# A decoder layer on one core: the router stage in another order, x1's low halves on VectorE, and x1's halves stored in plain column order

## The chip, the cores and the metric

The kernel runs on one core of a Trainium2 chip. A core has five engines with an instruction queue each: TensorE (PE; its weight loads are listed apart as PEld), VectorE (DVE), ScalarE (ACT), GpSimd (POOL) and SyncE (SP, which here issues nearly all DMA transfers). Each engine works through its own queue in program order; semaphores make an engine wait for another. The metric is the device time of one execution in microseconds (us). Most executions of one kernel lie close together, and a difference under 2% is hard to tell from none.

## What is computed

The reference is one layer of a decoder for 512 tokens of width 1024, in float32: a mixer of mLSTM heads and windowed attention, a residual with layer norm, and a mixture of 32 experts in 4 groups (the best group, then the best two experts in it), again with a residual and a layer norm.

```python
def reference(x, w_in, conv_w, conv_b, mlstm_gate_bias, mlstm_norm_w, attn_sinks, w_out,
...
        y = hybrid_mixer(x, w_in[l], conv_w[l], conv_b[l], mlstm_gate_bias[l], mlstm_norm_w[l],
                         attn_sinks[l], w_out[l])
        x = layer_norm(ALPHA * x + y, ln1_w[l], ln1_b[l])
        y = hierarchical_moe(x, w_group_router[l], b_group_router[l], w_expert_router[l],
                             b_expert_router[l], w_exp_gate[l], w_exp_up[l], w_exp_down[l])
        x = layer_norm(ALPHA * x + y, ln2_w[l], ln2_b[l])
...
    e_in = jnp.take_along_axis(e_logits, g_idx[:, None, None], axis=1)[:, 0]
    top_v, top_i = lax.top_k(e_in, TOP_K_INNER)
...
    for e in range(N_EXPERTS):
        h = jax.nn.silu(xt @ w_exp_gate[e]) * (xt @ w_exp_up[e])
        out = out + combine[:, e:e + 1] * (h @ w_exp_down[e])
```

## The kernel before, in words

Tokens are held in four blocks of 128 (`c` = 0 to 3), one token to a partition. The program has three parts: the mixer, the **router stage**, and thirteen **passes** over the experts.

**Router stage** (in the trace from about 201 to 266 us). For each block, TensorE multiplies the mixer's output by `w_out` in float32 kept as a high and a low half, three matmuls for a product: `out_mm` and, for the last rows of block 3, `ml_late`, each call being six matmuls of 512 columns. `norm_a` and `norm_b` make the residual and the layer norm, shared among VectorE, ScalarE and GpSimd by the table `NB`; the result is the tile `x1[c]`, 128 x 1024. `route_t` transposes it on TensorE, `route_m` multiplies by the router's weights, `route_d` (issued in pieces by `rd`) finds the best group and experts on VectorE, and `route_r` (by `rr`) counts with a small matmul where each token goes. `first_hot(c)` then writes on VectorE a 0/1 table `oh0` that says which token of block `c` goes to which of 256 places, and `first_pick(c, gs)` multiplies with it: the rows of `x1` are gathered by matmul into `xp`, transposed on the way. This gather is called a **pick**: weights are 128 columns of `x1`, the moving operand is 256 columns of the table.

To keep the value exact, a pick is done twice, with `x1h` (x1 rounded to the format of the fast matmul) and with `x1l` (what rounding left). `x1_hi` makes the first on ScalarE, `x1_lo` the second on GpSimd, both through `x1_parts`. The picks want every eighth column of `x1` as one group of 128 weights. So before the change ScalarE and GpSimd **read** `x1` with a step of eight columns (32 bytes) and **write** the halves regrouped, in the order (j, q):

```python
        v = x1[c].rearrange("p (q j) -> p j q", j=8)
...
                t.append(slot(n, F32R)[:, :DM].rearrange("p (j q) -> p j q", j=8))
```

so that a pick's weights `w[c][:, 2 * g + j2]` lie side by side.

The order of all this on TensorE, VectorE, GpSimd and ScalarE is the order of the calls in the program, written out by hand (`with tc.manual_schedule(engines=MAN)`); nothing moves them but that list.

**Passes.** A pass works on 128 places, shared by two or four experts (`ORDER`). `gu_part` multiplies by the gate and up weights (`we`), `dn_t` transposes the hidden values (its weights are read with a step of two columns, `h.rearrange("p (q j) -> p j q", j=2)`, line 1127), `dn_mm` multiplies by the down weights. Every second pass, `taken` (through `pairs_x`) gathers the tokens of the next two passes, with 64 picks; there are six such groups, and 64 more picks in the router stage. The weights, 3 MB an expert, stream from memory through a ring of 16 buffers and two lent ones; a buffer is refilled when its pass has used it. The experts of passes 0 to 2 are fixed; those of later passes are known at the end of the router stage (`slots_a`, `slots_e`).

The output rows of passes 0 to 7 are written to memory and fetched later by `y_fetch` and `y_add`; those of later passes are added to `x1` by a matmul and VectorE (`add_back`). The residual's factor `ALPHA` is put on `x1` by four GpSimd operations (line 1525) at the end of the router stage.

Of the kernel before, what the change touches and what calls it, by code (L numbers as in the profile page):

```python
# [11 lines left out]
F32R = mybir.dt.float32r  # L12
# [11 lines left out]
NCH = 4  # L24
# [54 lines left out]
def layer_kernel(ctx, tc, x, w_in, conv_w, conv_b, gate_bias, norm_w, sinks, w_out, ln1_w, ln1_b,  # L79
# [825 lines left out]
    def x1_hi(c, halves=None):  # L905
        for hi, _, v in x1_parts(c, halves):
            A.activation(hi, v, AF.Copy)

    def x1_lo(c, halves=None, eng=G):
        for hi, lo, v in x1_parts(c, halves):  # L910
            eng.tensor_tensor(lo, v, hi, op=OP.subtract)
# [270 lines left out]
    def add_back(o, y, cs=range(NCH)):  # L1182
        for c in cs:
            for u in range(2):
# [4 lines left out]
                V.tensor_add(x1[c][:, us], x1[c][:, us], b)  # L1189
# [198 lines left out]
    with tc.manual_schedule(engines=MAN):  # L1388
# [26 lines left out]
        rd(0, 4)  # L1415
        rd(0, 9)
        rr(0, 1)
        x1_hi(0)
        route_t(1, (0,))
        x1_hi(1)  # L1420
        close_pool("wr"); open_ring("ring1", NR // 2, "left"); prefetch(NR // 2); xs = xs_tiles()
        out_mm(2, 0, (0,), (2, 3))
        route_t(1, (1,))
        route_m(1, (0,))
        x1_lo(0)
        rr(0, 9)
        route_m(1, (1,))
        out_mm(2, 0, (1,), (0, 1))
        par(first_hot(0))
        norm_a(2, (0,))  # L1430
        rd(1, 4)
        first_pick(0, (0,))
        rd(1, 4)
        rr(1, 1)
        out_mm(2, 0, (1,), (2, 3))
        x1_lo(1)
        ml_late(3, ((0, 0), (1, 0)))
        rd(1, 9)
        rr(1, 9)
        ml_late(3, ((2, 0), (3, 0)))  # L1440
        par(first_hot(1))
        ml_late(3, ((0, 1), (1, 1)))
        ml_late(3, ((2, 1), (3, 1)))
        first_pick(0, (1,))
        norm_a(2, (1,))
        norm_b(2, 0)
        first_pick(1, (0,))
        norm_a(3, (0,))
        norm_b(2, 1)
        first_pick(0, (2,))  # L1450
        norm_a(3, (1,))
        route_t(2, (0,))
        route_t(2, (1,))
        norm_b(3, 0)
        route_m(2, (0,))
        norm_b(3, 1)
        route_m(2, (1,))
        x1_hi(2)
        rd(2, 4)
        route_t(3, (0,))  # L1460
        rd(2, 4)
        route_t(3, (1,))
        route_m(3, (0,))
        rr(2, 1)
        route_m(3, (1,))
        rd(2, 9)
        x1_hi(3, (0,))
        first_pick(1, (2,))
        x1_lo(2)
        x1_hi(3, (1,))  # L1470
        first_pick(0, (3,))
        first_pick(1, (1,))
        rr(2, 9)
        x1_lo(3, (1,), G)
        rd(3, 4)
        first_pick(1, (3,))
        rd(3, 4)
        par(first_hot(2))
        rr(3, 1)
        first_pick(2, (3,))  # L1480
        first_pick(2, (2,))
        slots_n()
        rd(3, 9)
        first_pick(2, (1,))
        x1_lo(3, (0,), G)
        rr(3, 9)
        first_pick(2, (0,))
# [36 lines left out]
    for c in range(NCH):  # L1524
        G.tensor_scalar(x1[c], x1[c], ALPHA, None, op0=OP.mult)
# [60 lines left out]
    with tc.manual_schedule(engines={ENG.PE, ENG.DVE}):  # L1586
        for p in range(2, NP - 1):
# [14 lines left out]
            if prev:  # L1602
# [3 lines left out]
                else:  # L1606
# [3 lines left out]
                    add_back(back(p - 1), y)  # L1610
# [197 lines left out]
```

## Time and profile before

| what | value |
|---|---|
| median of 3 runs | 532.84 us (529.39 to 538.61) |
| the profiled execution's own time | 534.1 us |
| its span, first to last instruction | 532.4 us |
| PE busy | 485.1 us, 91% of the span |
| DVE busy | 284.6 us, 53% |
| ACT busy | 161.3 us, 30% |
| POOL busy | 152.2 us, 29% |
| DMA, mean over the span | 252 GB/s |

Shares of busy time are means over parts with different limits, so the table says only where to look. A matmul's end is modelled, and matmuls overlap, so PE is read by the distance from one start to the next. From about 270 to 480 us the DMA engines are busy nearly all the time; before that they have long pauses.

### The profile page before, as it was taken

To read this page: it belongs to the slowest core of one execution; us is meant where nothing else is said; L and a number is where in the kernel's file an instruction comes from. 1 tells how busy PE (TensorE), PEld (TensorE's weight loads), DVE (VectorE), ACT (ScalarE), POOL (GpSimd) and SP (SyncE) were. 2 spreads that over 40 slices of the span, in tenths; PEclk is the share of its full clock that TensorE was granted. 3 is DMA by queue.
4 is the path that set the end of the run, shared out by engine and by line. 5 is a ranking of instruction groups with operands and counts; after the bars stand their busy time and mean duration, and the time that the engine had idled before them with its cause. 6 is when DMAs were issued, how large, how long until landed. Compare 5 with 4: busy or idle time off the path is not lost. (4 is left out here: it accounts for less than half of the span.)

```text
span 532.4 us, 8435 instructions
## 1 busy us (share of the span) xinstructions
PE 485.1 (91%) x3048; PEld 331.4 (62%) x3048; DVE 284.6 (53%) x636; ACT 161.3 (30%) x350; POOL 152.2 (29%) x177
## 2 busy tenths in 40 slices
PE   6999899999999999978899999899897988988881
PEld 5999688879889977767735563262632643553320
DVE  3543697974387675688973313030130464449953
ACT  3552565785534421504411111111111201012310
POOL 5479905322201102635810000000010120240531
PEclk9999999999999999989799999999999978989896
DMA  8724212221974538287569999999999999999030
GB/s 230 209 83 121 76 41 84 75 80 51 372 250 119 196 122 248 62 333 254 222 207 370 372 369 415 388 421 408 398 412 422 422 417 422 419 420 379 15 158 20
DMA packets 44462, 134.20 MB, mean 252 GB/s; under 512 B 6718, under 2 KB 17998, under 8 KB 41088
## 3 DMA queue, kind: packets, MB, share of 16 engines
q1 hardware_dynamic: 41504, 126.04, 63.2%
q0 software_dynamic: 2912, 7.58, 4.0%
q8 instruction: 25, 0.41, 0.3%
q14 instruction: 21, 0.17, 0.1%
HBM read 126.58 MB, written 8.91 MB: 255 GB/s over the span
## 5 line engine op out<-in xcount | busy, mean ns | idle before, releaser
L1106 PE MATMUL pg<-we,xs 128*32 128x512 f32 (+1 forms) x608 | 98.9, 604 | 7.4 <-DMA we<-in_w_exp_up 7.4
L1106 PEld LDWEIGHTS pg<-we,xs 128*32 128x32 f32 (+1 forms) x608 | 27.7, 121 | 65.6 <-issue 61.4
L244 PE MATMUL pj<-wh,xh 128*128 128x256 f32 (+1 forms) x224 | 63.7, 286 | 0.9 <-ACT wh L189 0.9
L245 PE MATMUL pj<-wh,xl 128*128 128x256 f32 (+1 forms) x224 | 62.8, 282 | 0.5 <-DVE xl L190 0.5
L1019 PE MATMUL xp<-ohr,x1h 128*128 128x256 f32 (+1 forms) x224 | 57.0, 295 | 1.7 <-DVE ohr L1014 1.7
L1019 PE MATMUL xp<-ohr,x1l 128*128 128x256 f32 (+1 forms) x224 | 55.7, 289 | 0.0
L249 PE MATMUL pj<-wl,xh 128*128 128x256 f32 x192 | 52.5, 280 | 0.0
L1019 PEld LDWEIGHTS xp<-ohr,x1h 128*128 128x128 f32 x224 | 44.5, 199 | 7.4 <-issue 4.9
L1137 PE MATMUL yo<-we,ht 128*32 128x512 f32 (+1 forms) x304 | 47.4, 595 | 0.5 <-DVE ht L1129 0.5
L1019 PEld LDWEIGHTS xp<-ohr,x1l 128*128 128x128 f32 x224 | 44.4, 198 | 0.0
L244 PEld LDWEIGHTS pj<-wh,xh 128*128 128x128 f32 x224 | 42.4, 189 | 1.3 <-ACT wh L189 1.1
L245 PEld LDWEIGHTS pj<-wh,xl 128*128 128x128 f32 x224 | 42.4, 189 | 0.7 <-DVE xl L190 0.7
L1155 POOL DMA_DIRECT2D yd<-y x8 | 4.4, 551 | 128.0 <-ACT y L1154 128.0
L1119 ACT ACTIVATE hid<-pg 128x256 f32<-128x256 f32 x13 | 5.0, 384 | 116.5 <-PE pg L1106 116.5
L1129 DVE COPY ht<-ph 128x256 f32<-128x256 f32 x13 | 5.5, 423 | 65.0 <-PE ph L1127 65.0
L249 PEld LDWEIGHTS pj<-wl,xh 128*128 128x128 f32 x192 | 35.6, 188 | 0.0
L190 DVE TENSOR_TENSOR wl<-wraw,wh 128x1024 fp32r<-128x1024 f32 x14 | 20.4, 1466 | 23.8 <-ACT wh L189 23.7
L1137 PEld LDWEIGHTS yo<-we,ht 128*32 128x32 f32 (+1 forms) x304 | 14.2, 119 | 27.1 <-issue 24.1
L1025 DVE COPY xs<-xp 128x512 f32<-128x512 f32 (+1 forms) x12 | 7.8, 647 | 38.1 <-PE xp L1019 38.1
L189 ACT ACTIVATE wh<-wraw 128x1024 fp32r<-128x1024 f32 (+2 forms) x23 | 23.2, 1021 | 12.3 <-PE pj L245 4.2
L1188 PE MATMUL cb<-yh,oh 128*128 128x512 f32 x32 | 18.6, 580 | 8.4 <-DVE oh L1176 6.2
L193 PE MATMUL pj<-xh,wh 128*128 128x512 f32 x64 | 25.7, 402 | 0.0
(352 smaller groups left out, 988.7 us busy)
## 6 DMA issues: line engine op xcount, KB each, us to landing
we<-in_w_exp_gate SPq DMA_DIRECT2D x64, 512.0 KB, 11.8
we<-in_w_exp_up SPq DMA_DIRECT2D x64, 512.0 KB, 11.9
we<-in_w_exp_down SPq DMA_DIRECT2D x26, 1024.0 KB, 12.9
wraw<-in_w_in SPq DMA_DIRECT2D x20, 512.0 KB, 3.4
we<-in_w_exp_down SPq DMA_DIRECT2D x12, 512.0 KB, 10.0
yd<-y POOLq DMA_DIRECT2D x8, 512.0 KB, 7.9
xc<-in_x SPq DMA_DIRECT2D x4, 512.0 KB, 9.2
wo<-in_w_out SPq DMA_DIRECT2D x8, 256.0 KB, 4.5
```

The costliest lines, as they stand in the source:

```text
L189: A.activation(hi, src, AF.Copy)
L190: eng.tensor_tensor(lo, src, hi, op=OP.subtract)
L193: TE.matmul(o, lh, rh, start=start, stop=False)
L244: TE.matmul(o, xh[j // 2][:, j % 2, cs], ws[i][j][0], start=j == 0, stop=False)
L245: TE.matmul(o, xl[j // 2][:, j % 2, cs], ws[i][j][0], start=False, stop=False)
L249: TE.matmul(o, xh[k // 2][:, k % 2, cs], ws[i][k][1], start=False, stop=k == 7)
L1019: TE.matmul(p_[:, j2, 0:P * n], w[c][:, 2 * g + j2], o[:, c, 0:P * n], start=c == 0 and s == 0 and j2 == 0, stop=c == NCH - 1 and s == 1 a ...
L1025: V.tensor_copy(d, p_[:, :, 0:P * n])
L1106: TE.matmul(pg[s:s + n], xs[k // 4][:, k % 4, P * b + s:P * b + s + n], ws[e][k // 4][:, :, k % 4], start=k == 0, stop=k == 7)
L1129: V.tensor_copy(ht, ph)
L1137: TE.matmul(py[u][s:s + n], ht[:, j, s:s + n], wt[e][2][j][:, 512 * u:512 * u + 512], start=j == 0, stop=j == 1)
L1188: TE.matmul(b, o[:, c * P:(c + 1) * P], t[:, us], start=i == 0, stop=i == 1)
```

## The change

Four things change. (1) `x1h` and `x1l` are written in the plain column order of `x1`; the step of eight moves to the picks, which now read their weights at columns 32 bytes apart. (2) `x1_lo` goes from GpSimd to VectorE. (3) The router stage's calls stand in another order: `out_mm` of block 2 and `ml_late` come earlier, the routing of block 1 later, and picks are grouped. (4) The four GpSimd multiplications by `ALPHA` go; the first `add_back` does the multiplication in the operation that adds.

```diff
-    def x1_parts(c, halves):
-        v = x1[c].rearrange("p (q j) -> p j q", j=8)
-        if len(x1h) == c:
-            for t, n in ((x1h, "x1h"), (x1l, "x1l")):
-                t.append(slot(n, F32R)[:, :DM].rearrange("p (j q) -> p j q", j=8))
-        for q in [slice(0, P)] if halves is None else [slice(64 * h, 64 * h + 64) for h in halves]:
-            yield x1h[c][:, :, q], x1l[c][:, :, q], v[:, :, q]
...
+    def x1_hi(c):
+        for t, n in ((x1h, "x1h"), (x1l, "x1l")):
+            t.append(slot(n, F32R)[:, :DM])
+        A.activation(x1h[c], x1[c], AF.Copy)
+
+    def x1_lo(c):
+        V.tensor_tensor(x1l[c], x1[c], x1h[c], op=OP.subtract)
...
-            TE.matmul(p_[:, j2, 0:P * n], w[c][:, 2 * g + j2], o[:, c, 0:P * n], start=c == 0 and s == 0 and j2 == 0,
+            TE.matmul(p_[:, j2, 0:P * n], w[c].rearrange("p (q j) -> p j q", j=8)[:, 2 * g + j2], o[:, c, 0:P * n], start=c == 0 and s == 0 and j2 == 0,
...
+                if first:
+                    V.scalar_tensor_tensor(x1[c][:, us], x1[c][:, us], ALPHA, b, op0=OP.mult, op1=OP.add)
+                else:
+                    V.tensor_add(x1[c][:, us], x1[c][:, us], b)
...
-        rd(0, 4)
-        rd(0, 9)
+        out_mm(2, 0, (0,), (2, 3))
+        rd(0, 19)
+        x1_hi(0)
+        out_mm(2, 0, (1,), (0, 1))
         rr(0, 1)
...
-    for c in range(NCH):
-        G.tensor_scalar(x1[c], x1[c], ALPHA, None, op0=OP.mult)
...
-                    add_back(back(p - 1), y)
+                    add_back(back(p - 1), y, first=p - 1 == KEPT)
```

How the list of calls moves is seen on the engines. **GpSimd**, from block 1's norm to the first pass. Names: `x_2217`, `x_2220`, `x_2223`, `x_2226` are `x1` of blocks 0 to 3; `lnmv` holds a norm's mean and scale; `l1w`, `l1b` are the norm's weights; `yd` is the passes' output in memory. Before:

```order
L895 TENSOR_TENSOR x_2220<-x_2220,l1b 128x512
L911 TENSOR_TENSOR x1l<-x_2217,x1h 128x1024
L911 TENSOR_TENSOR x1l<-x_2220,x1h 128x1024
L198 TENSOR_SCALAR lnmv<-lnmv 128x1
L199 TENSOR_TENSOR lnmv<-lnmv,mhalf 128x1
...
L911 TENSOR_TENSOR x1l<-x_2223,x1h 128x1024
L911 TENSOR_TENSOR x1l<-x_2226,x1h 128x8x64 x2
L1525 TENSOR_SCALAR x_2217<-x_2217 128x1024
...
L1525 TENSOR_SCALAR x_2226<-x_2226 128x1024
L1155 DMA yd<-y 128x1024 x7
```

and now:

```order
L895 TENSOR_TENSOR x_2220<-x_2220,l1b 128x512
L198 TENSOR_SCALAR lnmv<-lnmv 128x1
L199 TENSOR_TENSOR lnmv<-lnmv,mhalf 128x1
L198 TENSOR_SCALAR lnmv<-lnmv 128x1
L199 TENSOR_TENSOR lnmv<-lnmv,mhalf 128x1
L892 TENSOR_SCALAR lnmv<-lnmv 128x1
L894 TENSOR_TENSOR x_2223<-x_2223,l1w 128x512
L895 TENSOR_TENSOR x_2223<-x_2223,l1b 128x512
L1147 DMA yd<-y 128x1024 x7
```

All five subtractions and all four multiplications are gone from GpSimd; what is left of it in this stage is norms.

**VectorE**, at the end of the router stage, from the last steps of block 2's placing to block 3's table `ohr` (the tile of `oh0`). `cola` holds the places, `rank` and `rkt` the counts. Before:

```order
L1012 TENSOR_SCALAR ohr<-iot,cola 128x256
L978 TENSOR_SCALAR rr<-rr 128x4
L1014 SCALAR_TENSOR_TENSOR ohr<-iot,cola,ohr 128x256
L995 TENSOR_TENSOR rkt<-rsc,lg 128x64
...
L1002 TENSOR_SCALAR over<-rank 128x2
L1004 TENSOR_TENSOR cola<-cola,over 128x2
L1012 TENSOR_SCALAR ohr<-iot,cola 128x256
L1014 SCALAR_TENSOR_TENSOR ohr<-iot,cola,ohr 128x256
```

and now:

```order
L903 TENSOR_TENSOR x1l<-x_2223,x1h 128x1024
L1004 TENSOR_SCALAR ohr<-iot,cola 128x256
L972 RECIPROCAL rr<-rr 128x4
L1006 SCALAR_TENSOR_TENSOR ohr<-iot,cola,ohr 128x256
L987 TENSOR_TENSOR rkt<-rsc,lg 128x64
...
L996 TENSOR_TENSOR cola<-cola,over 128x2
L903 TENSOR_TENSOR x1l<-x_2226,x1h 128x1024
L1004 TENSOR_SCALAR ohr<-iot,cola 128x256
L1006 SCALAR_TENSOR_TENSOR ohr<-iot,cola,ohr 128x256
```

A subtraction of 128 x 1024 (line 903) now stands ahead of each block's table.

**TensorE**, where block 2's transposes (`rt<-ident,x_2223`) begin. `xp` is written by picks, `lg` by the router's and the counting matmuls, `py` by `out_mm` and `ml_late`. Before:

```order
L195 MATMUL py<-wol,mls 128x512
L1019 MATMUL xp<-ohr,x1h 128x256
L1019 MATMUL xp<-ohr,x1l 128x256
...
L923 MATMUL rt<-ident,x_2223 128x128 x8
L932 MATMUL lg<-rb,triu 128x40
L934 MATMUL lg<-rsc,x1T 128x40 x8
L923 MATMUL rt<-ident,x_2226 128x128 x8
```

and now:

```order
L195 MATMUL py<-wol,mls 128x512
L924 MATMUL lg<-rb,triu 128x40
L926 MATMUL lg<-rsc,x1T 128x40 x8
L1011 MATMUL xp<-ohr,x1h 128x256
L1011 MATMUL xp<-ohr,x1l 128x256
...
L983 LDWEIGHTS stril
L983 MATMUL lg<-ohs,stril 128x32
L985 LDWEIGHTS onesb
L985 MATMUL lg<-ohs,onesb 128x32
L915 MATMUL rt<-ident,x_2223 128x128 x4
```

Block 1's router matmuls and its count, which stood among the `py` matmuls, now stand behind the last of them, and all of block 0's picks but four stand between the two.

## Rows read from the trace of the kernel before

**Rows 1.** Windows by stage: two halves of the router stage, then the passes.

```profile
core 0: us, PE busy (x) PEld busy (x) DVE busy (x) ACT busy (x) POOL busy (x), PEclk, DMA share, GB/s
219.00:242.00 23.00, 19.17 (x92) 15.18 (x92) 19.26 (x46) 6.58 (x8) 12.76 (x9) 0.93 0.61 229
242.00:266.00 24.00, 19.90 (x134) 17.87 (x134) 20.98 (x59) 10.27 (x22) 17.43 (x11) 0.79 0.71 263
290.00:470.00 180.00, 167.96 (x1114) 85.40 (x1112) 50.65 (x106) 22.94 (x42) 15.64 (x20) 0.97 1.01 407
```

**Rows 2.** Waits of PE from 290 to 500 us: total us, times, longest.

```profile
PE pg L1106 <- DMA we<-in_w_exp_up: 7.4, 4, 2.6
```

**Rows 3.** Timeline of PE, first and last of 64 picks in a pass (start, us).

```profile
345.31 0.39 PE L1019 MATMUL xp<-ohr,x1h 128*128 128x256 f32 x1
...
352.93 0.29 PE L1019 MATMUL xp<-ohr,x1l 128*128 128x256 f32 x1
```

**Rows 4.** Weight loads of lines 1019, 1127 and 923: ns min/median/max.

```profile
L1019 PEld LDWEIGHTS xp<-ohr,x1h x224: 186/188/336, 230.2 to 468.9; 128*128 128x128 f32 x112
...
L1127 PEld LDWEIGHTS ph<-ident,hid x26: 194/208/219, 279.2 to 513.9; 128*128 128x128 f32 x26
...
L923 PEld LDWEIGHTS rt<-ident,x x32: 138/140/224, 213.2 to 248.0; 128*128 128x128 f32 x32
```

**Rows 5.** ScalarE's copies at lines 907 and 189: ns min/median/max.

```profile
L907 ACT ACTIVATE x1h<-x x5: 1153/2107/2202, 221.0 to 253.3; 128x1024 fp32r<-128x1024 f32 x3, 128x512 fp32r<-128x512 f32 x2
...
L189 ACT ACTIVATE wh<-wraw x23: 637/1059/1067, 5.5 to 144.2; 128x1024 fp32r<-128x1024 f32 x20, 128x792 fp32r<-128x792 f32 x2, 128x528 fp32r<-128x528 f32 x1
```

**Rows 6.** Timeline of GpSimd in the router stage.

```profile
223.30 3.07 POOL L911 TENSOR_TENSOR x1l<-x,x1h 128x1024 fp32r<-128x1024 f32 x1
226.81 3.06 POOL L911 TENSOR_TENSOR x1l<-x,x1h 128x1024 fp32r<-128x1024 f32 x1 [0.44 <-ACT x1h L907]
...
257.65 11.10 POOL L1525 TENSOR_SCALAR x<-x 128x1024 f32<-128x1024 f32 x4
```

**Rows 7.** Timeline of VectorE: the same operations beside GpSimd's and alone.

```profile
227.10 3.05 DVE L1014 SCALAR_TENSOR_TENSOR ohr<-iot,cola,ohr 128x256 fp32r<-128x256 f32 x1
...
231.86 0.16 DVE L948 TENSOR_TENSOR ohg<-iot,gi 128x4 f32<-128x4 f32 x1
...
234.92 0.48 DVE L1014 SCALAR_TENSOR_TENSOR ohr<-iot,cola,ohr 128x256 fp32r<-128x256 f32 x1
...
247.99 2.34 DVE L948 TENSOR_TENSOR ohg<-iot,gi 128x4 f32<-128x4 f32 x1
```

**Rows 8.** VectorE's subtraction of 128 x 1024 at line 190, in plain order.

```profile
L190 DVE TENSOR_TENSOR wol<-wo,woh x8: 1194/1218/1222, 164.4 to 195.0; 128x1024 fp32r<-128x1024 f32 x8
```

**Rows 9.** Timeline of PE: router matmuls, then a block of six matmuls, and the next.

```profile
218.43 0.98 PE L934 MATMUL lg<-rsc,x1T 128*128 128x40 f32 x8
219.24 0.48 PE L193 MATMUL py<-woh,mls 128*128 128x512 f32 x1
...
220.72 0.39 PE L193 MATMUL py<-woh,ams 128*128 128x512 f32 x1
```

**Rows 10.** Timeline of VectorE: first and last step of block 1's routing, a norm's step.

```profile
231.40 0.16 DVE L943 MAX8 gms<-lg 128x8 f32<-128x8 f32 x1
...
233.07 0.19 DVE L962 TENSOR_TENSOR ohs<-rsc 128x32 bf16<-128x32 f32 x1
...
238.02 0.75 DVE L888 SCALAR_TENSOR_TENSOR x<-x,lnmv,l1w 128x512 f32<-128x512 f32 x1
```

**Rows 11.** Timeline of VectorE, PE and SP at the end of the router stage.

```profile
261.98 0.48 DVE L1014 SCALAR_TENSOR_TENSOR ohr<-iot,cola,ohr 128x256 fp32r<-128x256 f32 x1
...
262.61 0.55 PE L1019 MATMUL xp<-ohr,x1h 128*128 128x256 f32 x1
...
265.36 0.22 PE L1241 MATMUL lg<-rsc 32*1 32x32 f32 x2
...
269.81 0.36 SPq L596 DMA_DIRECT2D we<-in_w_exp_gate  x1
```

More of the change, by code (lines that the diff above doesn't have):

```diff
@@ L895, in norm_b @@
             G.tensor_add(xh_, xh_, l1b[:, hs])
-    def x1_parts(c, halves):
-        v = x1[c].rearrange("p (q j) -> p j q", j=8)
-        if len(x1h) == c:
-            for t, n in ((x1h, "x1h"), (x1l, "x1l")):
-                t.append(slot(n, F32R)[:, :DM].rearrange("p (j q) -> p j q", j=8))
-        for q in [slice(0, P)] if halves is None else [slice(64 * h, 64 * h + 64) for h in halves]:
-            yield x1h[c][:, :, q], x1l[c][:, :, q], v[:, :, q]
[L905 to L911, printed above, removed]
+    def x1_hi(c):
[4 more added lines that the diff above has]
+        V.tensor_tensor(x1l[c], x1[c], x1h[c], op=OP.subtract)
     xts = {}
@@ L1180, in toks, with add_back @@
         return [t[:, p:p + 1] for t in tok2]
-    def add_back(o, y, cs=range(NCH)):
+    def add_back(o, y, cs=range(NCH), first=False):
         for c in cs:
@@ L1188, in add_back @@
                     TE.matmul(b, o[:, c * P:(c + 1) * P], t[:, us], start=i == 0, stop=i == 1)
-                V.tensor_add(x1[c][:, us], x1[c][:, us], b)
+                if first:
+                    V.scalar_tensor_tensor(x1[c][:, us], x1[c][:, us], ALPHA, b, op0=OP.mult, op1=OP.add)
+                else:
+                    V.tensor_add(x1[c][:, us], x1[c][:, us], b)
     q = C.tile([P, 5, 8], F32, name="slq")
@@ L1429, in layer_kernel @@
[L1429 to L1433, printed above, removed]
+        out_mm(2, 0, (1,), (2, 3))
+        norm_a(2, (0,))
+        x1_hi(1)
+        ml_late(3, ((0, 0), (1, 0)))
+        ml_late(3, ((2, 0), (3, 0)))
+        par(first_hot(0))
+        norm_a(2, (1,))
+        route_t(1, (0,))
+        ml_late(3, ((0, 1), (1, 1)))
+        route_t(1, (1,))
+        ml_late(3, ((2, 1), (3, 1)))
+        norm_a(3, (0,))
+        norm_b(2, 0)
+        norm_a(3, (1,))
@@ L1434, in layer_kernel @@
+        norm_b(2, 1)
+        route_m(1, (0,))
+        route_m(1, (1,))
+        first_pick(0, (0, 1, 2))
+        rd(1, 19)
+        norm_b(3, 0)
+        norm_b(3, 1)
         rr(1, 1)
-        out_mm(2, 0, (1,), (2, 3))
+        route_t(2, (0,))
+        first_pick(0, (3,))
+        route_t(2, (1,))
         x1_lo(1)
-        ml_late(3, ((0, 0), (1, 0)))
-        rd(1, 9)
         rr(1, 9)
-        ml_late(3, ((2, 0), (3, 0)))
+        route_m(2, (0,))
         par(first_hot(1))
-        ml_late(3, ((0, 1), (1, 1)))
@@ L1443, in layer_kernel @@
[L1443 to L1456, printed above, removed]
+        route_t(3, (0,))
         route_m(2, (1,))
         x1_hi(2)
-        rd(2, 4)
-        route_t(3, (0,))
-        rd(2, 4)
         route_t(3, (1,))
+        first_pick(1, (0, 1))
@@ L1463, in layer_kernel @@
         route_m(3, (0,))
+        rd(2, 19)
+        route_m(3, (1,))
+        x1_hi(3)
+        first_pick(1, (2, 3))
         rr(2, 1)
[L1465 to L1468, printed above, removed]
+        rd(3, 10)
+        rr(2, 9)
         x1_lo(2)
[L1470 to L1477, printed above, removed]
         par(first_hot(2))
@@ L1479, in layer_kernel @@
         rr(3, 1)
-        first_pick(2, (3,))
-        first_pick(2, (2,))
         slots_n()
-        rd(3, 9)
-        first_pick(2, (1,))
-        x1_lo(3, (0,), G)
+        first_pick(2)
         rr(3, 9)
-        first_pick(2, (0,))
+        x1_lo(3)
         par(first_hot(3))
```

7 lines of the change are left out of this document (removed).

## The prediction

> **What bounds the kernel now.** I read the windows by stage first. In the router stage neither the DMA engines nor any single engine is full: of 47 us from 219 to 266, PE is busy 39.1, and the granted clock falls to 0.93 and 0.79 [rows 1]. There the chain of waits counts. In the passes the picture is another one: from 290 to 470 us the DMA share is 1.01 and PE is busy 168 of 180 us at a clock of 0.97 [rows 1]. Both are full at once. The list of waits says how little room PE has there: it waits for expert weights four times, 7.4 us in all [rows 2]. So time that is added to PE's work in the passes is hidden for 7.4 us at most, and beyond that it is added to the kernel. That is the fact the forecast turns on.
>
> At the end of the router stage the last table of block 3 begins at 261.98 us and takes 0.48; the last sixteen picks follow at 262.61, the matmul that gives the experts' numbers at 265.36, and the first weights of a later expert are asked for at 269.81, when pass 0 has freed a buffer [rows 11]. Whatever moves 265.36 moves all that follows.
>
> **The change, part by part.**
>
> *The weights read with a step of eight.* There are 448 picks: 64 in the router stage, 64 in each of six groups in the passes. In a group, 64 picks start between 345.31 and 352.93, so one takes (352.93 - 345.31) / 63 = 0.121 us [rows 3], of which 256 moving columns fill nearly all; a load of 128 weights in plain order lasts 188 ns [rows 4] and lies beside the matmul ahead of it, overlapping the next load too. The trace has no load with a step of eight, so I bound it.
> - From below: the load gets no longer, or by so little that the matmul still hides it: 0 per pick. Nothing excludes that; a gain is excluded, as the matmuls' own columns stay.
> - The nearest row on PE itself is the transpose of line 1127, whose weights have a step of two: 208 ns against 140 for the transposes of line 923, same shape, plain order [rows 4]. So a step of two already costs 68 ns.
> - The nearest row with a step of eight is on ScalarE: the copy of 128 x 1024 takes 2107 ns with the step and 1059 without [rows 5], 1.02 ns more per element and partition. For 128 weights that is 131 ns.
>
> Both rows speak of a price, one because of the engine, the other because of the step. As a load now paces picks about as closely as the matmul does, what it gets longer comes on top of 0.121. I take the middle of the two, **100 ns a pick**; the ends 68 and 131 go into the range.
>
> The Trainium skill (SBUF — State Buffer, the note on cachelines under "Door 1: The DMA port swizzle") says that SBUF is read in lines of 16 bytes and that each access on a new line pays a penalty, so that fp32 may stride by up to four for free. That speaks against this change: 32 bytes puts each weight on a line of its own. The trace agrees for the step of eight on ScalarE and not for the step of two on PE, which by the rule would be free and is not. By the rule the step of eight has a price, but it gives no figure; taken at ScalarE's, the kernel would come to 575 us, at that of the row of line 1127 to 548.
>
> In the passes: 6 x 64 x 0.100 = 38.4 us on PE. Of that the waits for weights can swallow 7.4 [rows 2]: while PE is slower the DMA gets ahead and then waits for buffers. Net **+31.0 us**.
>
> *x1h in plain order.* ScalarE's copies fall from 2107 to about 1059 ns [rows 5]; ScalarE is busy 17 of 47 us in this stage [rows 1], so this pays only where a pick waits for the half, and I count nothing.
>
> *x1l on VectorE.* Four subtractions of 1.22 us [rows 8], 4.9 us in all, are added to an engine that is busy 40.2 of 47 us [rows 1]. In exchange GpSimd loses five subtractions (3.07 us for a block) and the multiplications by `ALPHA` (11.10 us) [rows 6]. That is worth more than GpSimd's time: VectorE's operations stretch while GpSimd runs these. The second step of a table takes 3.05 us beside a subtraction and 0.48 alone; the `ohg` step 2.34 and 0.16 [rows 7]. Two rows alone lose 4.8 us, as much as the four subtractions cost. The tail of the stage runs beside the `ALPHA` operations, so it gains there too. The multiplication itself goes into eight adds of the same shape in `add_back`: nothing.
>
> *The new order.* I walked the new list with the durations of the trace, every engine in its order. PE is at 222.1 us when the last attention part of block 3 ends, as before. Then seven blocks of six matmuls at 1.4 us (220.72 - 219.24 is one and a small gap) [rows 9], block 1's transposes 0.9 and its router matmuls 1.9 (0.98 a half) [rows 9]: 234.7. Block 0's table and halves are long done, its twelve picks take 1.5. Block 1's routing on VectorE takes 1.9 (231.40 to 233.26) [rows 10], to 237.2. Queued behind it are block 3's four norm steps, 0.75 each [rows 10], the middle ones held by GpSimd's two remaining norm operations on block 2: 241.9. Block 1's count waits behind these, and so do its x1l and table: 244.9. Block 2's routing, 246.9; its count stands on PE behind block 1's sixteen picks and block 3's router matmuls: 248.8. Block 3's routing ends at 251.1, and then VectorE has two counts, two subtractions and two tables in a row, 5.9 us: 257.0, against 262.46 (261.98 + 0.48) [rows 11]. So with free loads the stage ends **5.5 us earlier**. With 100 ns a pick, block 1's sixteen picks ahead of the count delay it by 1.6, the last sixteen take 1.6 more, and block 2's, partly hidden by VectorE, 0.4: +3.6. Net **-1.9 us**. What is late next is VectorE: in the new order it is the engine without pause, and TensorE waits for it three times (before the counts of blocks 2 and 3 and the last picks). Buffers and DMA issues keep their order on SP, and nothing on SP or GpSimd is moved past a transfer.
>
> *Sum*, made against the profiled execution (534.1 us, 1.3 above the median): -1.9 + 38.4 - 7.4 = **+29.1 us**. On the median, 532.84 + 29.1 = **562 us**, 5.5% slower. With 68 ns a pick: stage -3.3, passes 26.1 - 7.4, together +15.4, 548 us. With 131 ns: stage -0.4, passes 50.3 - 7.4, +42.5, 575 us.
>
> **The rivals.**
>
> *A, the load stays hidden.* If reading 128 weights at a step of eight still fits into the 0.121 us between picks, the passes stay as they are and the stage's 5.5 us are gained: 532.8 - 5.5 = 527 us, not slower. For it: the row of a step of two comes from a short pair of transposes, in which nothing long runs to hide a load, while picks hide theirs under 256 columns, and the rows of picks show loads overlapping. Against it: ScalarE's copy, which is a long stream, doubles; and at 0.121 us the load's 128 reads have hardly slack. The point from which it decides: with e us added per pick, the sum is -5.5 + 36 e in the stage (3.6 us for 0.1) plus 384 e less the 7.4; it is zero at e = 0.031, and +10.7 us (2%) at 0.056. The Trainium skill (TensorE: Matmul & The Clock Gate, "LDWEIGHTS (loading the stationary operand)") gives a load's time by its number of columns alone, and by that rule A would hold; the rows of lines 1127 and 923, equal in columns and different in time, don't agree.
>
> *B, free loads and a packed stage.* PE idles 7.9 us between 219 and 266 us, and the low clock (0.93 of 23, 0.79 of 24) is worth another 6.6 [rows 1]. If the loads are free and the new order closes most of these gaps, up to 14.5 us are gained, 518 us; over 10.7 would be faster by 2%. My walk leaves TensorE waiting three times for VectorE, so I give it little.
>
> *C, a dearer load.* If every access waits longer than on ScalarE, say twice its price (262 ns), the passes grow by 93 us after the 7.4, some 630 us. No row points there.
>
> **How the numbers follow.** The main case (68 to 131 ns, 548 to 575 us) gets 0.70, C 0.06, A 0.18, B 0.06. The likeliest is the main case, 562 us. A and B hold more than 2 in 10 together, so the range has to reach to A: it is 526 to 579, a little beyond A and beyond the upper price. Within 2% (543 to 522 us), about what a measurement of this kernel can tell from no change, lies A: 0.18. Faster by more is B: 0.06. Slower by more: 0.76.
>
> **What would show it.** Weight loads of picks at some 290 ns or more and picks some 0.22 us apart in the passes would show the main step right; loads near 188 ns and 0.121 would show A. The waits for expert weights (7.4 us) should be gone or nearly so. In the stage, the table steps should take 0.48 us throughout and the matmul for the experts' numbers should start near 263.5 us (near 260 under A). The prediction is wrong if the load's extra time is hidden, if the passes have room on PE that the list of waits doesn't show, or if the new order leaves TensorE waiting so long that its clock falls more often than before.

## The result, and the profile after

The kernel became slower: 573.56 us (571.82 to 573.83, 4 runs) against 534.56 us (529.39 to 538.61, 4 runs) for the kernel before on the same chip, a ratio of 1.0728, 95% interval 1.0676 to 1.078. The forecast was 562 us in a range of 526 to 579. (Here and below ratios leave disturbed executions out and medians do not, so a ratio need not be the quotient of two medians.)

To see where the 39 us lie I split each profiled execution at two instructions. The first is the second norm statistic of the router stage, VectorE's line 879, which stands ahead of everything the change touches; the second is TensorE's matmul for the experts' numbers, [rows 11], from which the passes run.

| us | before | after | difference | forecast |
|---|---|---|---|---|
| start to the norm statistic | 215.03 | 216.85 | +1.8 | 0 |
| router stage from there | 50.33 | 49.72 | -0.6 | -1.9 |
| passes, to the end of the span | 267.0 | 304.9 | +37.9 | +31.0 |
| span | 532.4 | 571.5 | +39.1 | +29.1 |

The first row is no effect of the change: in the fourteen profiles of this study that point lies anywhere from 215.0 to 220.0 us, with the same code ahead of it. Small effects in the stage are therefore read from the second row, not from the span.

The lines that answer to [rows 4]: weight loads and matmuls of the picks in the kernel after, nanoseconds as minimum/median/maximum.

```profile
L1011 PEld LDWEIGHTS xp<-ohr,x1h x224: 313/339/343, 236.9 to 505.7; 128*128 128x128 f32 x112
...
L1011 PEld LDWEIGHTS xp<-ohr,x1l x224: 334/338/347, 237.1 to 506.0; 128*128 128x128 f32 x112
```

The line of a load went from 188 to 339 ns. What that does to the pace is seen in TensorE's timeline of the kernel after: first and last pick of the first group in the passes, then of the last group, whose matmuls have only 128 moving columns (start, us).

```profile
291.78 0.52 PE L1011 MATMUL xp<-ohr,x1h 128*128 128x256 f32 x1
...
307.12 0.40 PE L1011 MATMUL xp<-ohr,x1l 128*128 128x256 f32 x1
...
490.89 0.46 PE L1011 MATMUL xp<-ohr,x1h 128*128 128x128 f32 x1
...
506.05 0.44 PE L1011 MATMUL xp<-ohr,x1l 128*128 128x128 f32 x1
```

(307.12 - 291.78) / 63 = 0.244 us a pick against 0.121 [rows 3]; the last group takes (506.05 - 490.89) / 63 = 0.241, with half the columns. So the load sets the pace now, and the columns don't matter. Before the change they mattered little too: there the last group's picks run from 461.95 to 469.04 us, 0.113 us each.

TensorE's waits of the kernel after in the passes (280 to 540 us), the answer to [rows 2]: total, times, longest. The wait for expert weights, 7.4 us before, is not in the list; these three are all of it.

```profile
PE cb L1180 <- DVE oh L1168: 6.0, 3, 2.2
PE cb L1180 <- DVE yl L1140: 1.7, 1, 1.7
PE cb L1180 <- DVE x L1184: 1.0, 2, 0.8
```

Windows by stage of the kernel after, as in [rows 1].

```profile
219.00:242.00 23.00, 23.00 (x118) 19.45 (x116) 18.49 (x46) 6.80 (x11) 8.42 (x10) 0.93 0.74 276
242.00:266.00 24.00, 18.91 (x110) 18.11 (x110) 14.97 (x65) 6.57 (x19) 0.56 (x1) 0.72 0.53 218
...
290.00:470.00 180.00, 177.63 (x949) 109.60 (x947) 38.65 (x84) 20.15 (x35) 12.22 (x16) 0.99 0.91 359
```

In the passes PE is busy 177.6 of 180 us and the DMA share has fallen from 1.01 to 0.91: two full resources have become one. In the stage GpSimd is relieved as forecast (9.0 us busy in 47, before 30.2), VectorE too (33.5, before 40.2), and yet the stage is hardly shorter. VectorE's timeline of the kernel after shows why: where the stage begins, a table step and an `ohg` step without stretching (compare [rows 7]), a subtraction, the count of block 1, and the wait of 5.03 us for the count of block 2.

```profile
216.85 0.21 DVE L879 BATCH_NORM_AGGREGATE lnmv<-lnst 128x2 f32<-128x12 f32 x1
...
230.51 0.48 DVE L1006 SCALAR_TENSOR_TENSOR ohr<-iot,cola,ohr 128x256 fp32r<-128x256 f32 x1
...
237.62 0.16 DVE L940 TENSOR_TENSOR ohg<-iot,gi 128x4 f32<-128x4 f32 x1
...
243.81 0.21 DVE L987 TENSOR_TENSOR rkt<-rsc,lg 128x64 f32<-128x64 f32 x1
243.94 1.22 DVE L903 TENSOR_TENSOR x1l<-x,x1h 128x1024 fp32r<-128x1024 f32 x1
...
253.57 0.22 DVE L987 TENSOR_TENSOR rkt<-rsc,lg 128x64 f32<-128x64 f32 x1 [5.03 <-PE lg L985]
```

### The profile page after: what moved, and what is told of

It reads as the page before. It is cut to its first block, busy times and chain, and to the rows that moved or that the text cites. A ratio compares the mean times of both kernels' runs of the same rounds, so it can differ in the third digit from the quotient of the medians.

```text
span 571.5 us, 8426 instructions
## 1 busy us (share of the span) xinstructions
PE 536.6 (94%) x3048; PEld 384.9 (67%) x3048; DVE 276.0 (48%) x640; ACT 156.9 (27%) x349; POOL 128.2 (22%) x168
## 5 line engine op out<-in xcount | busy, mean ns | idle before, releaser
L1098 PE MATMUL pg<-we,xs 128*32 128x512 f32 (+1 forms) x608 | 95.1, 600 | 0.0
L1011 PE MATMUL xp<-ohr,x1h 128*128 128x256 f32 (+1 forms) x224 | 93.6, 418 | 0.0
L1011 PE MATMUL xp<-ohr,x1l 128*128 128x256 f32 (+1 forms) x224 | 92.2, 412 | 0.0
L1011 PEld LDWEIGHTS xp<-ohr,x1h 128*128 128x128 f32 x224 | 75.6, 338 | 5.0 <-issue 4.9
L1011 PEld LDWEIGHTS xp<-ohr,x1l 128*128 128x128 f32 x224 | 75.8, 338 | 0.0
L1129 PE MATMUL yo<-we,ht 128*32 128x512 f32 (+1 forms) x304 | 50.0, 614 | 0.5 <-DVE ht L1121 0.5
L1129 PEld LDWEIGHTS yo<-we,ht 128*32 128x32 f32 (+1 forms) x304 | 14.8, 124 | 29.1 <-issue 26.0
L1019 ACT COPY xs<-xp 128x512 f32<-128x512 f32 (+1 forms) x16 | 9.0, 560 | 76.1 <-PE xp L1011 76.1
```

The costliest lines, as they stand in the source:

```text
L1011: TE.matmul(p_[:, j2, 0:P * n], w[c].rearrange("p (q j) -> p j q", j=8)[:, 2 * g + j2], o[:, c, 0:P * n], start=c == 0 and s == 0 and j2 == 0,
L1019: A.copy(d, p_[:, :, 0:P * n])
L1098: TE.matmul(pg[s:s + n], xs[k // 4][:, k % 4, P * b + s:P * b + s + n], ws[e][k // 4][:, :, k % 4], start=k == 0, stop=k == 7)
L1129: TE.matmul(py[u][s:s + n], ht[:, j, s:s + n], wt[e][2][j][:, 512 * u:512 * u + 512], start=j == 0, stop=j == 1)
```

## The experiments

Two theories stood. *The step*: reading 128 weights with a step of eight more than doubles the time of a pick, and that alone is the loss; the rest of the change gains little. Its rivals: the loss, or part of it, comes from the new order (TensorE waits and its clock falls), or from the x1 halves being read and written elsewhere. A second question came up with the first result: why the stage's gain stayed out. Experiments 1 to 4, 5 to 8, 9 to 11 and 12 ran on four chips, each group beside the kernel before on the same chip; a stage is read from one profile of each kernel.

**1. The kernel after, its picks without the step.**

```diff
-            TE.matmul(p_[:, j2, 0:P * n], w[c].rearrange("p (q j) -> p j q", j=8)[:, 2 * g + j2], ...
+            TE.matmul(p_[:, j2, 0:P * n], w[c][:, 128 * (2 * g + j2):128 * (2 * g + j2) + P], ...
```

> The changed kernel, with one thing undone: a pick reads 128 columns that lie side by side, so the experts get the wrong columns of x1 (routing, sizes and the list of instructions are the same). Theory 1 (the step of eight in the weight loads is the whole loss): weight loads back to 188 ns, picks 0.121 us apart, 46.9 us less on PE in the passes, the 7.4 us of waits for weights back; the kernel at 525 to 533 us. Theory 2 (the new order and the work given to VectorE lose a good part, the loads only some of it): 540 us or more.

Measured: 533.69 us (10 runs), ratio 0.999 (0.9944 to 1.0036). A load, the wait in the passes and the second window of the stage in this run's trace, and VectorE's wait for block 2's count:

```profile
L1011 PEld LDWEIGHTS xp<-ohr,x1h x224: 186/188/337, 238.4 to 472.3; 128*128 128x128 f32 x112
```
```profile
PE pg L1098 <- DMA we<-in_w_exp_up: 7.3, 4, 2.5
```
```profile
242.00:266.00 24.00, 17.28 (x88) 16.32 (x89) 14.55 (x56) 5.20 (x17) 1.99 (x2) 0.53 0.58 239
```
```profile
258.93 0.22 DVE L987 TENSOR_TENSOR rkt<-rsc,lg 128x64 f32<-128x64 f32 x1 [6.81 <-PE lg L985]
```

Load (188 ns), pace (0.120 us) and the wait for weights (7.3 us) are those of before within 0.001 us a pick and 0.1 us of waiting: the step is the whole loss, as far as an interval of about half a per cent either way can tell. The time lies 0.7 us above the 525 to 533 expected, since the stage gained nothing: with free loads the stage takes 51.2 us, not 5.5 us less than 50.3. The granted clock is 0.53 in its second half, and VectorE waits 6.8 us for one count. (The profiled execution took 537.3 us, 3.6 above the median of the ten. Experiment 3, with the same order, has a stage of 48.5 us; what differs is told below, with the account of the stage.)

**2. The kernel before, with nothing but the halves in plain order and the stepped read.** Order, engines and `ALPHA` stay as they were.

```diff
-        v = x1[c].rearrange("p (q j) -> p j q", j=8)
...
-                t.append(slot(n, F32R)[:, :DM].rearrange("p (j q) -> p j q", j=8))
+                t.append(slot(n, F32R)[:, :DM])
...
-            TE.matmul(p_[:, j2, 0:P * n], w[c][:, 2 * g + j2], ...
+            TE.matmul(p_[:, j2, 0:P * n], w[c].rearrange("p (q j) -> p j q", j=8)[:, 2 * g + j2], ...
```

> The kernel before, in its own order, with GpSimd still making x1l and multiplying by ALPHA; only the halves are stored in plain column order and the picks read their weights with a step of eight. Theory 1: picks 0.244 us apart, and 39 to 46 us slower than before, 573 to 580 us; a little slower than the changed kernel, since the order and VectorE's share bring back a few us there. Theory 2: well below the changed kernel, under 560 us.

Measured: 572.59 us (4 runs), ratio 1.0732 (1.0626 to 1.0837).

```profile
L1018 PEld LDWEIGHTS xp<-ohr,x1h x224: 312/338/347, 233.7 to 505.5; 128*128 128x128 f32 x112
```

The stepped read alone brings the same loss in the old order: the rival that blames the order falls from both sides. It came out no slower than the changed kernel, where a few us were expected from the order. The rival that blames where the halves are read and written falls with experiment 1, which has them in plain order and takes the time of before.

**3 and 4. The kernel after with a step of two, and of four.** One line of `pick` again, `[..., 2 * (P - 1) + 1:2]` and `[..., 4 * (P - 1) + 1:4]` in place of the step of eight.

> The changed kernel with a step of two in the weight loads of the picks (wrong columns of x1 reach the experts). If the price goes by lines of 16 bytes that a load touches (128 for a step of four or more, 64 for a step of two), a load needs about half of 0.244 us, which the 256 moving columns hide: loads longer than 188 ns (some 200 to 256), picks at 0.121 to 0.13 us, the kernel near 530 us. If any step costs the same, picks stay at 0.244 us and the kernel at 573 us.

> The changed kernel with a step of four, 16 bytes, in the weight loads of the picks (wrong columns of x1 reach the experts). By lines of 16 bytes each weight is on a line of its own, as with eight: picks at 0.244 us, the kernel near 573 us. If a step of up to four is free, picks at 0.121 us and the kernel near 530 us. If the price grows with the distance, something between.

Measured: 536.69 us and 572.79 us (one run each; the kernel before, 13 runs with these, 536.73). Step two, a load, and eleven picks in a row of a pass:

```profile
L1011 PEld LDWEIGHTS xp<-ohr,x1h x224: 192/197/337, 239.1 to 471.4; 128*128 128x128 f32 x112
```
```profile
315.63 0.29 PE L1011 MATMUL xp<-ohr,x1h 128*128 128x256 f32 x1
...
316.85 0.28 PE L1011 MATMUL xp<-ohr,x1h 128*128 128x256 f32 x1
```

Step four, a load, and the first and last pick of a group:

```profile
L1011 PEld LDWEIGHTS xp<-ohr,x1h x224: 308/331/339, 238.3 to 505.1; 128*128 128x128 f32 x112
```
```profile
294.59 0.51 PE L1011 MATMUL xp<-ohr,x1h 128*128 128x256 f32 x1
...
309.48 0.40 PE L1011 MATMUL xp<-ohr,x1l 128*128 128x256 f32 x1
```

A step of two costs 9 ns a load, and 0.122 us a pick: it stays hidden. A step of four costs 331 ns and (309.48 - 294.59) / 63 = 0.236 us, nearly all that a step of eight costs. The price is a stair between two and four elements, not a slope.

**5. Experiment 1 with idle matmuls.** 25 matmuls on `ident` whose result nobody reads: 9 ahead of the second half of block 2's transposes, 8 ahead of block 3's counts and 8 behind them. This asks whether the clock took the stage's gain.

```diff
+            TE.matmul(pls[c][:, 384:512], ident, ident, start=True, stop=True)
...
+        keep_warm(2, 9)
         route_t(2, (1,))
...
+        keep_warm(3, 8)
         rr(3, 1)
+        keep_warm(3, 8)
```

> The changed kernel with side-by-side columns in the picks (as in the first experiment, so the experts get wrong columns), and idle matmuls whose result nobody reads in three places of the router stage where TensorE waited: 9 ahead of block 2's second transposes, 8 ahead of block 3's count, 8 behind it. Theory: the stage's gain was lost to the low clock (0.53 from 242 to 266 us in the first experiment); with the clock kept up, the stage, measured from block 1's norm (the end of its statistics) to the matmul for the experts' numbers, falls from 51.2 us to 46 to 48. Rival: the order is the cause (block 2's count stands behind sixteen picks and block 3's router matmuls, VectorE waits 6.8 us for it), and the stage stays at 50 us or more although the clock is up.

Measured: 525.95 us (one run; before, 536.01 over 19 runs with it); stage 45.6 us against 51.2. The window that read 0.53:

```profile
242.00:266.00 24.00, 20.89 (x166) 17.00 (x165) 14.62 (x73) 8.25 (x21) 0.00 (x0) 1.00 0.46 188
```

More work on TensorE, and the stage is 5.6 us shorter than in experiment 1, 2.9 shorter than in experiment 3; the one run lies 3.5 us under the fastest of the 19 of before (529.45). The low clock had eaten the gain. Two of the three groups of idle matmuls stood in the way all the same: they waited for the bank that they write and then took 2.05 us ahead of work that was due (each matmul counts as two).

```profile
251.34 2.05 PE L927 MATMUL lg<-ident 128*128 128x128 f32 x16 [1.56 <-ACT gls L966]
...
254.68 2.05 PE L927 MATMUL lg<-ident 128*128 128x128 f32 x16 [1.20 <-DVE rkt L995]
```

**6. Experiment 1 with block 2's counts moved ahead of block 3's second router half.** No idle matmuls; `rr(2, 1)`, `rr(2, 9)`, `x1_lo(2)` and the table move up three calls.

> The first experiment's kernel (wrong columns reach the experts) with one move: block 2's count, x1l and table stand ahead of block 3's router matmuls and of block 1's last eight picks. No idle matmuls. If the place of the count is what cost the stage its gain, the wait of VectorE of 6.8 us goes, and the stage falls from 51.2 us to 45 to 47, and the clock may rise by itself as TensorE waits less. If the low clock is the cause, 50 us or more.

Measured: 532.22 us (one run), stage 46.0 us. VectorE's wait for the count of block 2:

```profile
253.38 0.22 DVE L987 TENSOR_TENSOR rkt<-rsc,lg 128x64 f32<-128x64 f32 x1 [2.04 <-PE lg L985]
```

It waits 2.0 us in place of 6.8. In experiment 1, eight picks and sixteen router matmuls stand right ahead of the count, from 252.65 to 258.52 us, 5.9 us, at 1.2 GHz (granted clock 0.50); here the eight picks and half of the router matmuls come behind it. But the clock rose in this profile too, to 0.79 in the same window and 1.00 from 252 to 254 us, right ahead of the count. So the place of the count and the clock moved together, and the share of each is not shown.

**7. The kernel before without GpSimd's `ALPHA`.** The multiplication goes into the first `add_back`, as in the change; nothing else.

> The kernel before with one part of the change: GpSimd's four multiplications by ALPHA go, the first add takes them over. Theory: the tail of the router stage loses its stretched VectorE steps, 2 to 4 us off the stage (50.3 us), the whole 0 to 4 us faster. Rival: those steps lie beside picks at the low clock, and nothing is gained.

Measured: 533.72 us (10 runs), ratio 0.9984 (0.9937 to 1.0031). In its profile the stage is 47.1 us, 3.2 less than before, as the theory had it; the time doesn't confirm it, as the interval runs from 0.6% faster to 0.3% slower, and a stage can differ by nearly as much between two profiles of one order (experiments 1 and 3). So a gain of this part by itself is not shown.

**8. The change without the stepped weights.** The halves are regrouped on the way in as before, but VectorE makes the low ones; order of the change, with the early counts of experiment 6. The whole computation.

```diff
-        A.activation(x1h[c], x1[c], AF.Copy)
+        A.activation(x1h[c], x1[c].rearrange("p (q j) -> p j q", j=8), AF.Copy)
...
-        V.tensor_tensor(x1l[c], x1[c], x1h[c], op=OP.subtract)
+        V.tensor_tensor(x1l[c], x1[c].rearrange("p (q j) -> p j q", j=8), x1h[c], op=OP.subtract)
```

> A full kernel: the changed one with the halves regrouped again, so that the picks read plain weights; ScalarE and VectorE read x1 with a step of eight to make them, and block 2's count is moved up as in the experiment before it. Theory: picks at 0.121 us; each regrouped copy costs ScalarE 1.05 us more and each subtraction VectorE some 1 us more, so the stage is 2 to 4 us longer than with wrong columns, 48 to 50 us; the kernel within 1% of the kernel before or up to 4 us faster. If VectorE reads a step of eight at full speed, 2 us better still.

Measured: 534.55 us (10 runs), ratio 0.9969 (0.9915 to 1.0023). The four subtractions and copies of the stage, grouped (busy us, mean ns), then two of TensorE's waits:

```profile
L900 ACT ACTIVATE x1h<-x 128x1024 fp32r<-128x1024 f32 x4 | 8.7, 2182 | 0.0
...
L903 DVE TENSOR_TENSOR x1l<-x,x1h 128x1024 fp32r<-128x1024 f32 x4 | 8.4, 2105 | 0.0
```
```profile
241.39 0.18 PE L983 MATMUL lg<-ohs,stril 128*128 128x32 bf16 x1 [1.63 <-ACT gls L958]
...
260.35 0.21 PE L983 MATMUL lg<-ohs,stril 128*128 128x32 bf16 x1 [3.75 <-ACT rex L966]
```

VectorE pays for the step as ScalarE does, 2105 ns against 1219. That is 3.5 us more in four subtractions; the stage takes 49.8 us against 46.0 in experiment 6. Both waits name ScalarE. But the second matmul doesn't read `rex`; it reads `ohs`, which VectorE finishes (line 954) at 260.29 us, 0.06 ahead of it. So there TensorE waits for VectorE.

**9. Experiment 8 with idle matmuls** (8 ahead of block 1's counts, 9 as in experiment 5, 24 and 2 around block 3's counts), written into the bank of the block whose turn it is.

> A full kernel: that of the eighth experiment (halves regrouped by reading x1 with a step of eight, block 2's count early) with idle matmuls where TensorE waits: 8 ahead of block 1's count, 9 ahead of block 2's second transposes, 24 ahead of block 3's count, 2 behind it. Theory: the low clock, there in the eighth experiment from 243 to 253 and 260 to 267 us, goes, and with it some 3 to 4 us of the stage (49.8 us): 46 to 47 us, the kernel 0.5 to 1.5% faster than the kernel before. If the stage stays at 49 us or more, the strided subtractions on VectorE are the limit and the clock is not.

Measured: 538.52 us (10 runs), ratio 1.0055 (1.0008 to 1.0102); stage 52.8 us. TensorE's timeline, the idle matmuls alone (each counts as two):

```profile
243.10 2.05 PE L927 MATMUL lg<-ident 128*128 128x128 f32 x16 [1.64 <-ACT gls L966]
...
245.98 2.17 PE L927 MATMUL lg<-ident 128*128 128x128 f32 x18
...
259.17 7.25 PE L927 MATMUL lg<-ident 128*128 128x128 f32 x48 [3.18 <-ACT gls L966]
```

A miss. The brackets show it: the idle matmuls themselves waited, 1.64 and 3.18 us, for ScalarE to have read that bank, then took their time on the path. They were also more than the pauses hold: 2.05 and 7.25 us, where experiment 8 waited 1.63 and 3.75 us, and the last 24 ran partly at a low clock themselves (0.68 from 259.2 to 262 us, 0.81 from there to 266.2).

**10. Experiment 9 with the regrouping on the writing side**: x1 is read in plain order, the halves are written with a step of 128 columns (VectorE also reads the high half with it).

> The same, but the regrouping is done on the writing side: ScalarE reads x1 in plain order and writes x1h with a step of 128 columns; VectorE reads x1h and writes x1l with that step. If only reading pays for a step, ScalarE's copy is back near 1.06 us and VectorE's subtraction lies between 1.2 and 2.1 us; if writing pays too, both stay at 2.1 us or more.

Measured: 539.25 us (one run).

```profile
L900 ACT ACTIVATE x1h<-x 128x1024 fp32r<-128x1024 f32 x4 | 8.1, 2035 | 0.2 <-POOL x L895 0.2
...
L903 DVE TENSOR_TENSOR x1l<-x,x1h 128x1024 fp32r<-128x1024 f32 x4 | 7.9, 1977 | 0.0
```

Writing with a step costs ScalarE within 7% of what reading with one costs. VectorE comes out the same way, but it still reads one input with the step here, so its price for writing alone is not shown.

**11. The kernel before, without `ALPHA` on GpSimd, with idle matmuls**: 12 ahead of block 1's counts, 10 ahead of block 2's, 9 around block 3's.

> The kernel before, in its order, without the multiplications by ALPHA on GpSimd (as in the seventh experiment), with idle matmuls ahead of the counts of blocks 1, 2 and 3 (12, 10, 3) and behind the last (6). Theory: its three spells of low clock go; the stage falls from 47.1 us in the seventh experiment to 43 to 45, the kernel 0.5 to 1.2% faster than the kernel before. Rival: GpSimd's subtractions still hold VectorE up, and the stage stays at 46 us or more.

Measured: 540.02 us (4 runs), ratio 1.0114 (1.0024 to 1.0205); stage 55.7 us.

```profile
233.11 2.94 PE L935 MATMUL lg<-ident 128*128 128x128 f32 x24 [1.36 <-DVE lg L959]
...
252.92 4.62 PE L935 MATMUL lg<-ident 128*128 128x128 f32 x20
```

The same miss as in experiment 9: the idle matmuls lie on the path. Ten of them at 1.2 GHz (granted clock 0.50 from 253 to 257.4 us) took 4.6 us ahead of a count.

**12. Experiment 8 with 24 idle matmuls in a bank that nobody reads** at the time, block 2's, 5, 7 and 12 of them.

```diff
+        keep_warm(2, 5)
         rr(1, 1)
...
+        keep_warm(2, 7)
         route_t(2, (1,))
...
+        keep_warm(2, 12)
         rr(3, 1)
```

> The whole computation: the kernel of e8_regrouped_count_early (halves regrouped as before the change, VectorE computing the low halves, block 2's expert counts ahead of block 3's router matmuls) with 24 idle matmuls, as in e9, but all of them written into block 2's logits bank at moments when no engine reads it: 5 ahead of block 1's counts, 7 ahead of the second half of block 2's transposes, 12 ahead of block 3's counts. Theory: the idle matmuls of e9 came late because the bank that they wrote was being read; put into a bank that nobody reads they start at once and end (5, 7 and 12 times 0.256 us = 1.3, 1.8 and 3.1 us) inside the gaps of 1.63, 1.86 and 3.75 us that e8's profile shows ahead of the same matmuls. Then TensorE's clock stays at 2.4 GHz, the stage takes 46 to 47.5 us in place of e8's 49.8, and the kernel is 0.3 to 1% faster than before the change (529 to 533 us). Rival: the gaps are not free, since the bank is still being read when the first of them come, or the idle matmuls at half clock take twice 0.256 us and delay the counts: stage 49.5 us or more, time within 0.5% of before.

Measured: 530.04 us (12 runs; before, 534.57 over 17), ratio 0.9906 (0.9865 to 0.9947); stage 45.9 us. TensorE's timeline, idle matmuls and the two counts behind them; then the window.

```profile
236.69 1.28 PE L927 MATMUL lg<-ident 128*128 128x128 f32 x10
238.48 0.18 PE L991 MATMUL lg<-ohs,stril 128*128 128x32 bf16 x1 [0.51 <-ACT gls L966]
...
239.53 1.72 PE L927 MATMUL lg<-ident 128*128 128x128 f32 x14
...
250.88 2.84 PE L927 MATMUL lg<-ident 128*128 128x128 f32 x24
254.81 0.19 PE L991 MATMUL lg<-ohs,stril 128*128 128x32 bf16 x1 [1.09 <-ACT rex L974]
```
```profile
242.00:266.00 24.00, 20.32 (x162) 16.25 (x159) 17.92 (x74) 10.47 (x21) 0.00 (x0) 1.00 0.44 182
```

They start at once, and the counts behind them still wait 0.51 and 1.09 us for others: the idle matmuls lie inside the gaps. The clock is 1.00, the stage 3.9 us shorter than in experiment 8, and the whole computation is 0.5 to 1.4% faster than before the change, by an interval that leaves out no difference, though under the 2% that are easy to tell from none. It keeps the change's order and VectorE's low halves, and leaves out its plain column order. From experiment 9 it differs in two things, the bank and the number of idle matmuls (24 in place of 43); no run takes them apart.

## Why the prediction was right, point by point

**Right: the step is what decides.** "The weights read with a step of eight" carried the sum, and experiments 1 and 2 show it from both sides: without it the changed kernel takes the time of before, and the old kernel with it takes the time of after.

**Mis-sized: the load's price.** "I take the middle of the two, 100 ns a pick": it measured 244 - 121 = 123 ns, near the upper end of 131. The row with the same step on another engine [rows 5] was the better guide, and the row with another step on the same engine [rows 4] the worse: experiment 3 has a step of two in picks at 197 ns against 188, so the 68 ns between lines 1127 and 923 are not the price of the step in such a stream. What makes up those 68 ns was not tried. 384 picks at 0.123 are 47.2 us instead of 38.4.

**Right: 7.4 us are swallowed.** The waits for weights are gone after the change and in experiment 2, and back at 7.3 in experiment 1. 47.2 - 7.4 = 39.8, measured 37.9; the granted clock from 290 to 470 us was 0.99 instead of 0.97 [rows 1], by estimate worth up to 3.6 of those 180 us, but nothing isolates it.

**Right in the parts, wrong in the sum: the stage.** The plain copies took 1064 ns, the subtractions 1.22 us, and the stretched rows fell to 0.48 and 0.16 us, all as forecast. The failing step is "I walked the new list with the durations of the trace": these were mostly durations at 2.4 GHz. The walk put block 1's count on VectorE 26.9 us behind the norm statistic (241.9 - 215.03). It was there at 243.81 - 216.85 = 27.0, and in experiment 1 at 27.0. Up to there the walk was exact. It put block 2's count at 33.8 with free loads. Experiment 1 had it at 258.52 - 218.36 = 40.2, experiment 3 at 255.85 - 219.09 = 36.8, and experiment 5, at full clock, at 249.54 - 215.33 = 34.2. So VectorE was not "the engine without pause" either: it waited for that count 5.03 us in the kernel after, 6.81 and 4.12 in experiments 1 and 3, and 2.84 in experiment 5.

What TensorE did before the clock fell is in the traces of experiments 1 and 3, which have the same order and picks of 0.120 and 0.122 us. In both it stood for 2.18 us, waiting for block 2's norm on GpSimd. Groups of four transposes, in experiment 1 ahead of that wait and behind it:

```profile
240.83 0.63 PE L915 MATMUL rt<-ident,x 128*128 128x128 f32 x4
...
244.12 1.11 PE L915 MATMUL rt<-ident,x 128*128 128x128 f32 x4 [2.18 <-POOL x L895]
```

and in experiment 3 behind it and once more, with the second window of the stage:

```profile
244.86 0.66 PE L915 MATMUL rt<-ident,x 128*128 128x128 f32 x4 [2.18 <-POOL x L895]
...
247.42 1.09 PE L915 MATMUL rt<-ident,x 128*128 128x128 f32 x4
```
```profile
242.00:266.00 24.00, 17.19 (x107) 16.32 (x106) 17.21 (x66) 5.74 (x18) 2.73 (x2) 0.72 0.62 251
```

In experiment 1 the low clock shows right behind the wait, in experiment 3 only by the next four transposes, and there it is up again ahead of block 2's count: the router matmuls and picks that take 5.9 us in experiment 1 take 255.85 - 252.61 = 3.2. So two profiles of one order differ in when the clock falls and rises, and with it in the stage, 51.2 and 48.5 us. Both are far from the walk's 44.8 (50.3 - 5.5). The named mishap, "the new order leaves TensorE waiting so long that its clock falls more often", came true, in the stage only.

The two terms of the stage then nearly cancelled, and one profile each is too little to size them. By experiment 1 the walk's -5.5 came out as +0.9 (51.2 against 50.3) and the +3.6 for slow picks as -1.5 (49.7 against 51.2); by experiment 3 as -1.9 and +1.3. Two things are seen to keep the slow picks from costing 3.6. They filled TensorE's pause: the wait of 2.18 us is 0.50 in the kernel after. And at the low clock the step costs little. The windows below go from the start of one pick to the start of a later one among the last picks of the stage, in the kernel after 13 picks and then 14, in experiment 1 13 picks.

```profile
259.05:262.20 3.15, 3.15 (x14) 3.15 (x14) 2.94 (x10) 0.00 (x0) 0.00 (x0) 0.50 0.00 0
262.63:266.00 3.37, 3.37 (x15) 3.37 (x15) 0.27 (x2) 1.46 (x3) 0.00 (x0) 1.00 0.02 5
```
```profile
264.40:267.17 2.77, 2.77 (x14) 2.77 (x14) 2.63 (x8) 0.00 (x0) 0.00 (x0) 0.50 0.00 0
```

With the step a pick takes 3.15 / 13 = 0.242 us at a granted clock of 0.50 (1.2 GHz) and 3.37 / 14 = 0.241 at 1.00 (2.4 GHz); without it 2.77 / 13 = 0.213 at 0.50 and 0.120 at 1.00. So the step's price is 0.03 us a pick at the lower level and 0.12 at the upper one, and "+3.6" had taken one price for all. A net of -1.9 forecast and -0.6 measured looks closer than the reasoning was: that is luck.

**The account of the miss.** From the profiled 534.1 us the forecast is 563.2, measured was 573.5: 6.9 us in the passes (8.8 from the price, less 1.9), 1.3 in the stage, 1.8 ahead of it, and 0.3 outside of the span. With one profile on either side, the 1.3 can't be told from what the stage differs by in two profiles of one order (2.7). That 573.56 lies within the range is owed to the upper price, of ScalarE's copy: the middle that the sum used was 0.023 us a pick too low.

**The rivals.** A (the load stays hidden) is false for a step of eight and true for a step of two: 0.001 us more a pick. Its decisive point, 0.031 us, lies between a step of two and one of four. B (a packed stage, up to 14.5 us) fell; the shortest stage of all runs is 45.6, 4.7 us less than before. C (a dearer load) fell, 151 ns more a load and 123 a pick being the whole price. Of the Trainium skill, the rule of 16-byte lines (SBUF — State Buffer, "Door 1: The DMA port swizzle"), by which fp32 may stride by up to four for free, holds for the step of two (0.122 us a pick) and not for the step of four (0.236), at which each weight already has a line of 16 bytes to itself. The formula by columns alone (TensorE: Matmul & The Clock Gate, "LDWEIGHTS (loading the stationary operand)") does not hold here: 188, 197, 331 and 339 ns are loads of the same 128 columns.

**Left open.** What inside the load makes the steps of four and eight cost the same, and that of eight the same at either clock; why the point ahead of the stage varies by 5 us between executions, and the moment at which the clock falls between two profiles of one order; and how much of experiment 12's gain belongs to the idle matmuls alone, since its interval and that of experiment 8 (0.9915 to 1.0023) overlap and only their profiled stages (45.9 and 49.8 us) stand apart.

## What to carry to other kernels

A layout's price is paid once, where the data is regrouped, or each time that it is read: the copies were about 1.1 us cheaper for each of four blocks, and 448 picks dearer, 384 of them by 0.12 us where only 7.4 us in all could hide it. When an operation is hidden behind another with no slack, price its growth in full, and take the price from the row with the same access pattern rather than from the same engine. A new order worked out with full-clock durations is not finished until every pause of TensorE in it has been looked at: either move what others wait for ahead of the long work behind the pause, or fill the pause with idle matmuls, no more than it holds and into a bank that nobody is reading (experiment 12 did both, and which of the two counts is not shown).

## What was not expected of the hardware

- The load's price jumps between a step of two and four: 188, 197, 331, 339 ns for steps of one, two, four and eight float32 elements. Picks of 256 and of 128 moving columns then run at the same 0.24 us (before, 0.121 and 0.113), and picks at a granted clock of 0.50 and of 1.00 as well (0.242 and 0.241), while plain ones differ (0.213 and 0.120).
- VectorE (1219 to 2105 ns) and ScalarE (1064 to 2182 ns) pay alike for reading 128 x 1024 with the step; ScalarE pays as much for writing with one (2035 ns), and VectorE for reading one input and writing with one (1977 ns).
- Adding 24 matmuls to TensorE shortened the profiled stage from 49.8 to 45.9 us; more of the same kind lengthened it to 52.8 us, and in the old order from 47.1 to 55.7 us, where they waited for their bank or stood ahead of a count that was due.
